# Score levels placed by one wide copy each and a re-ordered start, in a streaming-encoder trunk

## The chip, the cores and the metric

The kernel runs on one core of a Trainium2 chip. The metric is the device time of one execution in microseconds (us), the median of several runs. TensorE is the matmul engine, VectorE and ScalarE the elementwise engines, GpSimd the fourth; the trace calls them PE, DVE, ACT and POOL. SP is the engine that issues most DMAs.

## The reference

Two layers of a streaming encoder on x (512 tokens, 1024 channels) in float32, cut here to what is computed:

```python
for l in range(DEPTH):                      # DEPTH = 2
    x = x + 0.5 * swiglu(rmsnorm(x, ffn1_norm[l]), ffn1_w1[l], ffn1_w3[l], ffn1_w2[l])
    h = rmsnorm(x, mix_norm[l])
    q_a, f_a, i_a, g_a, u_b = jnp.split(h @ w_in[l], splits, axis=-1)
    o_a = hgrn2_mixer(q_a, f_a, i_a, g_a, lb_all[l], hgrn_norm[l])   # gated linear recurrence, 4 heads
    o_b = multiscale_pool(u_b, pool_w[l], pool_scale[l])             # trailing means over 2, 4, 8, 16
    x = x + jnp.concatenate([o_a, o_b], axis=-1) @ w_out[l]
    x = x + mem_cross_attention(rmsnorm(x, xa_norm[l]), rmsnorm(mem, mem_norm[l]), ...)
    x = x + 0.5 * swiglu(rmsnorm(x, ffn2_norm[l]), ffn2_w1[l], ffn2_w3[l], ffn2_w2[l])
return rmsnorm(x, final_norm)
```

The recurrence is S_t = diag(f_t) S_(t-1) + k_t v_t^T with o_t = S_t^T q_t; inside a stretch of tokens it is a masked product of scores with v.

## The kernel before, in words

All activations are held transposed: eight x tiles of 128 channels by 512 tokens. Every matrix operand is split into a high part (`whi`, `h`) and a low part (`wlo`), and a product is three matmuls (`mm3`, lines 84 to 86): high by high, high by low, low by high. `split` (lines 76 to 80) makes the high part on ScalarE and the low part on VectorE.

Weights come in chunks (`Weights`): 512 KB of raw weights are loaded on SP's queue (`load`, line 142), split (`cut`), and used by 24 matmuls of 512 columns. `next` hands out a chunk, cuts those `ahead` (SPLIT = 5 of them) and loads those 7 ahead. Tiles for all this, and for most of the rest, come from one pool of 38 slots (`s_tile`).

The feed-forward networks treat their first chunks plainly and the rest in blocks (`Pairs.block`): two chunks taken together by a scheme with seven products, for which sums of weights are needed. A block's load (lines 128 to 135) is four DMAs on SP's queue and one accumulating DMA on GpSimd's (`wsum`), its cut four splits and two additions (eight slots), and each of its products is closed by a copy on ScalarE (`keep`, line 545). A block counts as two in `ahead`.

At the start, x is loaded in five DMAs with chunk 0 (in halves) and chunk 1 between them. Eleven dummy products (line 1134) run on a tile of ones. `wts.first()` cuts chunk 0, `norm.part(d)` splits each x tile (lines 79 and 80), and `begin` multiplies chunks 0 to 3 with the x tiles, two tiles (a `k2`) at a time; the squares of x (lines 386 and 392), which the norm needs, come from its fourth step on. The norm's row is applied when a PSUM tile is evacuated.

In the mixing stage (`mix`) the scores inside stretches of 128 tokens are built level by level: at level m (1, 2, 4, ... 64) the first half of each stretch of 2m tokens meets the second half. `levels` is a generator that is stepped between weight chunks. At levels 2 to 16 `dense` forms products (line 768) for the two groups g of heads, ScalarE copies them to `packed` (line 777), DMAs on ScalarE's queue put them into `spread` (line 782), which is zero elsewhere, and `place` writes them by `copy_predicated` into the score tile `atd` (line 740), eight instructions of 64 elements for a group. At level 32 eight copies evacuate the products (line 773), at level 64 one for a group (line 816). After each level, `kg` and `qf` are scaled in place for the next one (lines 822 and 824), and a level is placed in the step of group 0 of the next.

The order of the instructions on each engine is set when the kernel is built: a planner walks the program with its own model of time and lets a later instruction go first where an earlier one is not ready.

Of the kernel before, what the change touches and what calls it, by code (L numbers as in the profile page):

```python
# [7 lines left out]
F32 = mybir.dt.float32  # L8
F32R = mybir.dt.float32r
I32 = mybir.dt.int32  # L10
AF = mybir.ActivationFunctionType
ALU = mybir.AluOpType
AX = mybir.AxisListType

P = 128
D = 1024
T = 512
M = 256
L = 2
NK = D // P  # L20
NT = T // P
# [25 lines left out]
def trunk_kernel(ctx: ExitStack, tc: tile.TileContext, ap: dict, out: bass.AP):  # L47
    nc = tc.nc
# [19 lines left out]
    def s_tile(shape, dt, name):  # L68
        return sp.tile(shape, dt, tag="s", name=name)


    def split(hi, lo, src, scale=None):


        if scale is None:
            act.copy(hi, src)  # L76
            dve.tensor_tensor(lo, src, hi.bitcast(F32), op=ALU.subtract)  # L77
        else:
            act.activation(hi, src, AF.Copy, scale=scale)
            dve.scalar_tensor_tensor(lo, src, scale, hi.bitcast(F32), op0=ALU.mult, op1=ALU.subtract)  # L80
# [8 lines left out]
    class Weights:  # L89
# [33 lines left out]
        def load(self, i):  # L123
            if i in self.raw or i in self.hl:
                return
            if len(self.src[i]) == 2:
                c1, c2 = self.src[i]
                s1, t1 = s_tile([P, NK, P], F32, "wsum"), s_tile([P, NK, P], F32, "raw")
                t2 = s_tile([P, 4, P], F32, "raw")
                nc.sync.dma_start(s1[:, :4], c1[:, :4])  # L130
                nc.sync.dma_start(s1[:, 4:], c2[:, :4])
                nc.sync.dma_start(t1, c1)
                nc.sync.dma_start(t2, c2[:, 4:])
                nc.gpsimd.dma_start(s1, c2, accum_op=ALU.add)
                self.raw[i] = [t.rearrange("p a b -> p (a b)") for t in (t1, t2, s1)]
                return
            src, a, b = self.src[i]
            t = s_tile([P, 1024], F32, "raw")
            tv = t[:, :a * b].rearrange("p (a b) -> p a b", b=b)
            for c in range(0, a, a if i else a // 2):  # L140
                ce = c + (a if i else a // 2)
                nc.sync.dma_start(tv[:, c:ce], src[:, c:ce])
            self.raw[i] = t

        def cut(self, i):
# [30 lines left out]
            _, a, b = self.src[i]  # L176
            hi, lo = s_tile([P, 1024], F32R, "whi"), s_tile([P, 1024], F32R, "wlo")
            n = a * b
            step = n if i else n // 2
            for c in range(0, n, step):  # L180
                split(hi[:, c:c + step], lo[:, c:c + step], raw[:, c:c + step])
            self.hl[i] = tuple(t[:, :n].rearrange("p (a b) -> p a b", b=b) for t in (hi, lo))
            yield

# [5 lines left out]
                else:  # L190
                    return

        def first(self):
            self.todo.append(self.cut(0))
            self.step()

        def next(self):
            i = self.at
            self.at += 1
            while self.todo:  # L200
                self.step()
            block = len(self.src[i]) == 2
            ahead = [*self.ahead(i, 4 if block else self.SPLIT)]
            if i + 3 == len(self.src) - 1:
                ahead.append(i + 3)
            for j in ahead:
                if j not in self.hl:
                    self.todo.append(self.cut(j))
                    if not block or j == i:
                        while self.todo:  # L210
                            self.step()
            for j in self.ahead(i, self.LOAD):
                self.load(j)
            return self.hl.pop(i)
# [41 lines left out]
    xT = [xall[:, d] for d in range(NK)]  # L256
    vec = const.tile([P, NV], F32, name="vec")
    nc.scalar.dma_start(vec, ap["vec"])
    for c, ce in ((0, 1), (1, 2), (2, 4), (4, 6), (6, 8)):
        nc.sync.dma_start(xall[:, c:ce], ap["x"][:, c:ce])  # L260
        if c % 2 == 0 and c < 4:
            wts.load(c // 2)

    fixed = const.tile([P, P + 16 + 64 * len(MASKS)], F32, name="fixed")
    nc.sync.dma_start(fixed, ap["fixed"])
# [424 lines left out]
    def mix(l, norm, mem, after):  # L690
# [41 lines left out]

        def place(g, m, rows):

            for hh in range(2):
                o = atd[g][:, hh].rearrange("p i (b e j) -> p i b e j", e=2, j=m)
                src = rows[:, hh * 256:(hh + 1) * 256].rearrange("p (i b j) -> p i b j", i=NT, j=m)
                mk = masks[m].rearrange("p (b j) -> p b j", j=m)
                for i in range(NT):
                    dve.copy_predicated(o[:, i, :, 1, :], mk, src[:, i])  # L740

        keys = [None, None]

# [9 lines left out]
                dst = keys[g][:, hh * HT:(hh + 1) * HT].rearrange("p (i j b) -> p i b j", i=NT, j=m)  # L753
                act.copy(dst, src[:, hh].rearrange("p (i b) j -> p i b j", i=NT))

        spread = s_tile([P, 2, T], F32, "spread")
        pool.memset(spread, 0.0)
        packed = [None]

        def dense(g, m):  # L760
# [17 lines left out]
            if g == 1:  # L778
                n = max(m, 64 // m)
                for x in range(64 // n):  # L780
                    rows = slice(x, P, 2 * m) if m <= 4 else slice(2 * m * x, 2 * m * x + m)
                    nc.scalar.dma_start(spread[rows], packed[0][x * n:(x + 1) * n])

        def levels():

# [7 lines left out]
            for m in (1, 2, 4, 8, 16, 32, 64):  # L793
                nb = T // (2 * m)
                tots = [None, None]
                for g in range(2):
# [19 lines left out]
                        dve.tensor_copy(atd[g][0:64, :, :, 64:128].rearrange("p h i t -> p (h i) t"),  # L816
                                        ps[0:64, :].rearrange("p (x t) -> p x t", t=64))
                    tv = tot[g].rearrange("p h (b e) -> p h b e", e=2)
                    kv = kg[g].rearrange("p h (b e j) -> p h b e j", e=2, j=m)
                    qv = qf[g].rearrange("p h (b e j) -> p h b e j", e=2, j=m)  # L820
                    for hh in range(2):
                        dve.tensor_tensor(kv[:, hh, :, 0, :], kv[:, hh, :, 0, :],
                                          tv[:, hh, :, 1:2].broadcast_to([P, nb, m]), op=ALU.mult)
                        dve.tensor_tensor(qv[:, hh, :, 1, :], qv[:, hh, :, 1, :],
                                          tv[:, hh, :, 0:1].broadcast_to([P, nb, m]), op=ALU.mult)
                    nt_ = s_tile([P, 2, nb], F32, "tot") if m == 1 else sm.tile([P, 2, nb], F32, tag=f"tot{m}", name="tot", bufs=2)
                    dve.tensor_tensor(nt_, tv[:, :, :, 0], tv[:, :, :, 1], op=ALU.mult)
                    tots[g] = nt_
                    if m < 32:
                        first_halves(g, 2 * m)  # L830
                    if g == 0 and 2 < m <= 32:
                        place(0, m // 2, spread[:, 0])
                        place(1, m // 2, spread[:, 1])
                    yield
                tot = tots
            last.extend(tot)
# [293 lines left out]


    idle = ps_tile()
    for _ in range(11):
        pe.matmul(idle[:, :P], ones, ones, start=True, stop=True)
    norm = Norm("ffn1_norm", 0, late=1, rest=0, far=0)
    wts.first()
    for d in range(NK):
        norm.part(d)

    def begin(norm):  # L1140

        ps = [ps_tile(), ps_tile(), acc_tile(), acc_tile()]
        w = {}
        for p, k2 in ((0, 0), (0, 1), (1, 0), (1, 1), (0, 2), (1, 2), (0, 3), (1, 3),
                      (2, 0), (2, 1), (2, 2), (2, 3), (3, 0), (3, 1), (3, 2), (3, 3)):
            if p not in w:
                w[p] = wts.next()
            for k in (2 * k2, 2 * k2 + 1):
                mm3(ps[p], (w[p][0][:, k], w[p][1][:, k]), norm.h[k], start=k == 0, stop=k == NK - 1)
            while norm.n < NK and p + k2 > 1:  # L1150
                norm.square(norm.n)
            if p == 2 and k2 == 2:
                norm.tick()
        return ps
# [80 lines left out]
```

## Time and profile before

| what | us |
|---|---|
| median of 3 runs | 2135.25 (2132.23 to 2136.88) |
| the profiled execution | 2134.99 |
| its span, from the first to the last instruction | 2133.2 |
| TensorE busy | 2106.7 |
| VectorE busy | 1370.6 |
| ScalarE busy | 901.2 |
| GpSimd busy | 225.5 |

The mean granted clock of TensorE over the span is 0.994 of full speed. The clock has two levels, 1.2 and 2.4 GHz, so a mean below 1 over a stretch is a share of it at the lower level. A matmul's row gives its duration from issue to a modelled end; neighbours overlap, so their spacing is read from their starts.

### The profile page before, as it was taken

How to read it: one execution, taken by the hardware profiler on the slowest of the kernel's cores; microseconds unless marked ns; L12 is line 12 of the kernel's file. 1: busy time of each engine (PE TensorE's matmuls, PEld its weight loads, DVE VectorE, ACT ScalarE, POOL GpSimd, SP SyncE). 2: the span in 40 equal slices, each digit the busy share in tenths (PEclk: the TensorE clock that was granted, in tenths of full speed). 3: DMA queues.
4: the chain of work that ended last, by engine and by line, in shares of the span. 5: the costliest groups of instructions: out<-in, count | busy, mean ns of one | idle time of the engine just before them, and what ended most of it. 6: DMA issues, size and time to landing. Idle time of an engine off the chain costs nothing. (4 is left out here: it accounts for less than half of the span.)

```text
span 2133.2 us, 31051 instructions
## 1 busy us (share of the span) xinstructions
PE 2106.7 (99%) x12380; PEld 1858.4 (87%) x12380; DVE 1370.6 (64%) x2104; ACT 901.2 (42%) x1397; POOL 225.5 (11%) x216
## 2 busy tenths in 40 slices
PE   9999999999999999999999999999999999999998
PEld 7889898887988888999988998988789888889896
DVE  6747565687646485755676575658875556657565
ACT  4425345433534343544444353434244443435254
POOL 1100000312000020000011000003110001100002
PEclk9999999999999999999999999999999999999999
DMA  4355465222424245737325745532334331475453
GB/s 176 107 158 149 119 170 167 68 86 95 143 79 138 62 113 144 190 104 193 127 57 151 193 119 164 167 104 73 86 110 133 109 104 50 140 202 133 135 154 117
DMA packets 106866, 271.58 MB, mean 127 GB/s; under 512 B 10592, under 2 KB 10592, under 8 KB 106720
## 3 DMA queue, kind: packets, MB, share of 16 engines
q1 hardware_dynamic: 92944, 227.85, 32.0%
q0 software_dynamic: 11952, 38.02, 10.2%
q10 hardware_dynamic: 1824, 3.73, 0.8%
q8 instruction: 97, 1.59, 0.3%
q14 instruction: 49, 0.40, 0.1%
HBM read 259.85 MB, written 2.10 MB: 123 GB/s over the span
## 5 line engine op out<-in xcount | busy, mean ns | idle before, releaser
L77 DVE TENSOR_TENSOR wlo<-raw,whi 128x1024 fp32r<-128x1024 f32 (+1 forms) x329 | 404.5, 1250 | 81.2 <-ACT whi L76 73.7
L76 ACT CAST whi<-raw 128x1024 fp32r<-128x1024 f32 (+1 forms) x329 | 335.0, 1046 | 118.3 <-DMA raw<-in_ffn_w_dram 57.3
L84 PE MATMUL ps<-h,whi 128*128 128x512 f32 x848 | 333.4, 395 | 5.1 <-DVE atd L773 4.1
L85 PE MATMUL ps<-h,whi 128*128 128x512 f32 x848 | 333.3, 393 | 0.5 <-DVE h L80 0.5
L86 PE MATMUL ps<-h,wlo 128*128 128x512 f32 x848 | 332.0, 392 | 0.4 <-DVE wlo L77 0.4
L84 PE MATMUL ps<-bh,whi 128*128 128x256 f32 x744 | 210.1, 284 | 3.4 <-ACT keep L545 2.8
L84 PE MATMUL acc<-bh,whi 128*128 128x256 f32 x744 | 211.1, 284 | 1.9 <-ACT keep L545 1.9
L85 PE MATMUL acc<-bl,whi 128*128 128x256 f32 x744 | 211.0, 284 | 0.0
L86 PE MATMUL acc<-bh,wlo 128*128 128x256 f32 x744 | 210.9, 284 | 0.0
L86 PE MATMUL ps<-bh,wlo 128*128 128x256 f32 x744 | 210.9, 283 | 0.0
L85 PE MATMUL ps<-bl,whi 128*128 128x256 f32 x744 | 210.8, 283 | 0.0
L77 DVE TENSOR_TENSOR wlo<-wsum,whi 128x1024 fp32r<-128x1024 f32 x124 | 154.9, 1249 | 69.3 <-ACT whi L76 68.1
L76 ACT CAST whi<-wsum 128x1024 fp32r<-128x1024 f32 x124 | 130.1, 1050 | 157.9 <-DVE wsum L164 85.5
L84 PEld LDWEIGHTS ps<-h,whi 128*128 128x128 f32 x848 | 160.9, 190 | 40.0 <-issue 4.3
L85 PEld LDWEIGHTS ps<-h,whi 128*128 128x128 f32 x848 | 160.9, 190 | 35.7 <-DVE h L80 2.5
L86 PEld LDWEIGHTS ps<-h,wlo 128*128 128x128 f32 x848 | 160.8, 190 | 34.5 <-DVE wlo L77 0.8
L84 PEld LDWEIGHTS ps<-bh,whi 128*128 128x128 f32 x744 | 142.6, 192 | 4.3 <-ACT keep L545 3.1
L84 PEld LDWEIGHTS acc<-bh,whi 128*128 128x128 f32 x744 | 143.2, 192 | 2.6 <-ACT keep L545 2.3
L85 PEld LDWEIGHTS acc<-bl,whi 128*128 128x128 f32 x744 | 143.3, 193 | 0.3
L85 PEld LDWEIGHTS ps<-bl,whi 128*128 128x128 f32 x744 | 143.0, 192 | 0.6
L86 PEld LDWEIGHTS acc<-bh,wlo 128*128 128x128 f32 x744 | 143.3, 193 | 0.0
L86 PEld LDWEIGHTS ps<-bh,wlo 128*128 128x128 f32 x744 | 143.0, 192 | 0.0
(262 smaller groups left out, 4295.4 us busy)
## 6 DMA issues: line engine op xcount, KB each, us to landing
raw<-in_ffn_w_dram SPq DMA_DIRECT2D x207, 512.0 KB
wsum<-in_ffn_w_dram SPq DMA_DIRECT2D x124, 256.0 KB
wsum<-in_ffn_w_dram POOLq DMA_DIRECT2D x62, 512.0 KB, 6.3
raw<-in_ffn_w_dram SPq DMA_DIRECT2D x64, 256.0 KB
raw<-in_w_in_dram SPq DMA_DIRECT2D x32, 512.0 KB
raw<-in_w_out_dram SPq DMA_DIRECT2D x16, 512.0 KB
raw<-in_xa_wk_dram SPq DMA_DIRECT2D x16, 512.0 KB
raw<-in_xa_wq_dram SPq DMA_DIRECT2D x16, 512.0 KB
```

What stands on the lines that cost most here:

```text
L76: act.copy(hi, src)
L77: dve.tensor_tensor(lo, src, hi.bitcast(F32), op=ALU.subtract)
L84: pe.matmul(o, a[0], b[0], start=start, stop=False, skip_group_check=more)
L85: pe.matmul(o, a[0], b[1], start=False, stop=False, skip_group_check=more)
L86: pe.matmul(o, a[1], b[0], start=False, stop=stop, skip_group_check=more)
```

## The change

- `load` and `cut` lose the special case of chunk 0. A new `half` loads or splits one half (four of eight row blocks) of a chunk. x is loaded with halves of chunks 0 and 1 between its DMAs, and their splits stand between the splits of x tiles 0 to 3.
- In `begin` the pairs alternate between chunk 0 and chunk 1 from the start, two dummy products stand after each of the first six pairs, and the squares come after the eighth. Thirteen dummies instead of eleven run first.
- `next` cuts 4 ahead instead of 5 as soon as one of the next four entries is a block.
- `place` is one instruction of 512 elements with the mask broadcast, the scalings of `kg` and `qf` take both heads of a group at once, `spread` has two buffers that alternate by level, and a level is placed in the step of group 1 of the next level, not of group 0.

```diff
@@ class Weights
+        def half(self, i, c, what):
+            src, a, b = self.src[i]
+            if i not in self.raw:
+                self.raw[i] = s_tile([P, 1024], F32, "raw")
+                self.hl[i] = tuple(s_tile([P, NK, P], F32R, x) for x in ("whi", "wlo"))
+            t = self.raw[i].rearrange("p (a b) -> p a b", b=b)[:, 4 * c:4 * c + 4]
+            if what == "load":
+                nc.sync.dma_start(t, src[:, 4 * c:4 * c + 4])
+            else:
+                hi, lo = self.hl[i]
+                split(hi[:, 4 * c:4 * c + 4], lo[:, 4 * c:4 * c + 4], t)
+                if c:
+                    self.raw.pop(i)
...
             block = len(self.src[i]) == 2
-            ahead = [*self.ahead(i, 4 if block else self.SPLIT)]
+            near = any(len(x) == 2 for x in self.src[i:i + 4])
+            ahead = [*self.ahead(i, 4 if near else self.SPLIT)]
...
-    for c, ce in ((0, 1), (1, 2), (2, 4), (4, 6), (6, 8)):
+    for c, ce, half in ((0, 1, 0), (1, 2, None), (2, 4, 1), (4, 6, None), (6, 8, None)):
         nc.sync.dma_start(xall[:, c:ce], ap["x"][:, c:ce])
-        if c % 2 == 0 and c < 4:
-            wts.load(c // 2)
+        if half is not None:
+            wts.half(0, half, "load")
+            wts.half(1, half, "load")
...
         def place(g, m, rows):
-            for hh in range(2):
-                o = atd[g][:, hh].rearrange("p i (b e j) -> p i b e j", e=2, j=m)
-                src = rows[:, hh * 256:(hh + 1) * 256].rearrange("p (i b j) -> p i b j", i=NT, j=m)
-                mk = masks[m].rearrange("p (b j) -> p b j", j=m)
-                for i in range(NT):
-                    dve.copy_predicated(o[:, i, :, 1, :], mk, src[:, i])
+            o = atd[g].rearrange("p h i (b e j) -> p (h i) b e j", e=2, j=m)[:, :, :, 1, :]
+            src = rows.rearrange("p (x b j) -> p x b j", x=2 * NT, j=m)
+            mk = masks[m].rearrange("p (o b j) -> p o b j", o=1, j=m).broadcast_to([P, 2 * NT, 64 // m, m])
+            dve.copy_predicated(o, mk, src)
...
-        spread = s_tile([P, 2, T], F32, "spread")
-        pool.memset(spread, 0.0)
+        spreads = [s_tile([P, 2, T], F32, "spread") for _ in range(2)]
+        for t in spreads:
+            pool.memset(t, 0.0)
+        spread = {m: spreads[i % 2] for i, m in enumerate((2, 4, 8, 16))}
...
-                    for hh in range(2):
-                        dve.tensor_tensor(kv[:, hh, :, 0, :], kv[:, hh, :, 0, :],
-                                          tv[:, hh, :, 1:2].broadcast_to([P, nb, m]), op=ALU.mult)
-                        dve.tensor_tensor(qv[:, hh, :, 1, :], qv[:, hh, :, 1, :],
-                                          tv[:, hh, :, 0:1].broadcast_to([P, nb, m]), op=ALU.mult)
+                    dve.tensor_tensor(kv[:, :, 0, :], kv[:, :, 0, :], tx[:, :, 1:2].broadcast_to([P, 2 * nb, m]), op=ALU.mult)
+                    dve.tensor_tensor(qv[:, :, 1, :], qv[:, :, 1, :], tx[:, :, 0:1].broadcast_to([P, 2 * nb, m]), op=ALU.mult)
...
-                    if g == 0 and 2 < m <= 32:
-                        place(0, m // 2, spread[:, 0])
-                        place(1, m // 2, spread[:, 1])
+                    if g == 1 and 2 < m <= 32:
+                        for x in range(2):
+                            place(x, m // 2, spread[m // 2][:, x])
...
-    for _ in range(11):
-        pe.matmul(idle[:, :P], ones, ones, start=True, stop=True)
+    def rest(n):
+        for _ in range(n):
+            pe.matmul(idle[:, :P], ones, ones, start=True, stop=True)
+    rest(13)
     norm = Norm("ffn1_norm", 0, late=1, rest=0, far=0)
-    wts.first()
     for d in range(NK):
         norm.part(d)
+        if d < 4:
+            wts.half(d % 2, d // 2, "split")
...
-        for p, k2 in ((0, 0), (0, 1), (1, 0), (1, 1), (0, 2), (1, 2), (0, 3), (1, 3),
+        for p, k2 in ((0, 0), (1, 0), (0, 1), (1, 1), (0, 2), (1, 2), (0, 3), (1, 3),
...
-            while norm.n < NK and p + k2 > 1:
+            if p < 2 and k2 < 3:
+                rest(2)
+            while norm.n < NK and p + k2 > 3:
                 norm.square(norm.n)
```

## Rows read from the trace of the kernel before

**Rows 1.** The page: busy us (share), instructions of each engine.

```profile
PE 2106.7 (99%) x12380; PEld 1858.4 (87%) x12380; DVE 1370.6 (64%) x2104; ACT 901.2 (42%) x1397; POOL 225.5 (11%) x216
```

**Rows 2.** Waits of TensorE: us in total, times, longest us.

```profile
PE ps L84 <- DVE atd L773: 4.1, 2, 2.0
PE ps L815 <- DVE qf L824: 3.2, 3, 1.1
PE ps L84 <- ACT keep L545: 2.8, 1, 2.8
PE acc L84 <- ACT keep L545: 1.9, 2, 1.0
```

**Rows 3.** Windows: us, each engine's busy us (instructions), TensorE's clock, DMA share, GB/s.

```profile
6.14:22.75 16.61, 15.33 (x48) 10.25 (x49) 14.36 (x24) 15.20 (x22) 0.00 (x0) 0.79 0.99 391
...
160.00:170.00 10.00, 10.00 (x79) 10.00 (x78) 4.09 (x8) 3.83 (x9) 1.72 (x2) 0.91 0.78 217
...
480.00:503.00 23.00, 18.79 (x111) 15.02 (x108) 20.79 (x57) 2.28 (x3) 6.30 (x13) 0.85 0.21 58
...
1530.00:1552.00 22.00, 18.80 (x122) 15.14 (x120) 20.51 (x59) 2.10 (x2) 6.30 (x13) 0.92 0.21 61
```

**Rows 4.** Timeline of TensorE, start: start us, duration us, [wait].

```profile
1.00 4.55 PE L1134 MATMUL ps<-ones 128*128 128x128 f32 x22 [1.00 <-POOL nhalf L277]
6.14 0.49 PE L84 MATMUL ps<-h,whi 128*128 128x512 f32 x1 [0.59 <-ACT h L79]
...
8.24 0.78 PE L84 MATMUL ps<-h,whi 128*128 128x512 f32 x1 [0.41 <-ACT h L79]
```

**Rows 5.** Timeline of ScalarE at the start.

```profile
7.47 0.72 ACT L79 ACTIVATE h<-xall,vec 128x512 fp32r<-128x512 f32 x1 [0.86 <-DMA xall<-in_x_dram]
...
11.63 1.33 ACT L79 ACTIVATE h<-xall,vec 128x512 fp32r<-128x512 f32 x2 [0.21 <-DMA xall<-in_x_dram]
...
15.13 1.04 ACT L76 CAST whi<-raw 128x1024 fp32r<-128x1024 f32 x1
```

**Rows 6.** Groups of VectorE, 0 to 24 us: busy us, mean ns, idle.

```profile
L80 DVE SCALAR_TENSOR_TENSOR h<-xall,vec,h 128x512 fp32r<-128x512 f32 x8 | 5.8, 746 | 0.8 <-ACT h L79 0.6
L392 DVE TENSOR_TENSOR sq<-sq 128x512 f32<-128x512 f32 x7 | 4.8, 684 | 0.2
```

**Rows 7.** Timelines of SP, GpSimd, ScalarE, TensorE at the first block entry.

```profile
142.38 0.33 SPq L130 DMA_DIRECT2D wsum<-in_ffn_w_dram  x1
...
147.14 0.86 POOL L134 DMA_DIRECT2D wsum<-in_ffn_w_dram  x1 [14.08 <-DVE xall L436]
...
156.34 1.04 ACT L76 CAST whi<-wsum 128x1024 fp32r<-128x1024 f32 x1 [5.96 <-issue]
157.29 0.64 ACT L545 COPY keep<-ps 128x256 f32<-128x256 f32 x2
...
157.70 0.39 PE L84 MATMUL ps<-bh,whi 128*128 128x256 f32 x1 [2.85 <-ACT keep L545]
```

**Rows 8.** TensorE after level 64, layer 0: first, last half-clock product.

```profile
494.06 0.77 PE L84 MATMUL ps<-h,whi 128*128 128x512 f32 x1 [2.04 <-DVE atd L773]
...
499.74 0.44 PE L85 MATMUL ps<-h,whi 128*128 128x512 f32 x1
```

**Rows 9.** Timelines of VectorE and ScalarE, levels 4 to 16 of layer 0.

```profile
457.64 2.27 DVE L740 COPY_PREDICATED atd<-fixed,spread 128x64 f32<-128x64 int32 x16 [1.87 <-DMA spread<-packed]
...
474.27 0.57 ACT L777 COPY packed<-ps 64x512 f32<-64x512 f32 x1
...
476.24 4.20 DVE L740 COPY_PREDICATED atd<-fixed,spread 128x64 f32<-128x64 int32 x16 [1.08 <-DMA spread<-packed]
...
480.51 2.46 ACTq L782 DMA_DIRECT2D spread<-packed  x4
```

**Rows 10.** Groups of VectorE in layer 0's mixing, and line 824's min/median/max ns.

```profile
L801 DVE TENSOR_TENSOR atd<-ps,fixed 128x512 f32<-128x512 f32 x4 | 2.6, 678 | 0.0
...
L824 DVE TENSOR_TENSOR qf<-qf,tot x48: 402/416/1264, 442.3 to 1551.2; 128x256 f32<-128x256 f32 x48
```

More of the change, by code (lines that the diff above doesn't have):

```diff
@@ L139, in load @@
             tv = t[:, :a * b].rearrange("p (a b) -> p a b", b=b)
-            for c in range(0, a, a if i else a // 2):
-                ce = c + (a if i else a // 2)
-                nc.sync.dma_start(tv[:, c:ce], src[:, c:ce])
+            nc.sync.dma_start(tv, src)
             self.raw[i] = t
@@ L178, in cut @@
             n = a * b
-            step = n if i else n // 2
-            for c in range(0, n, step):
-                split(hi[:, c:c + step], lo[:, c:c + step], raw[:, c:c + step])
+            split(hi[:, :n], lo[:, :n], raw[:, :n])
             self.hl[i] = tuple(t[:, :n].rearrange("p (a b) -> p a b", b=b) for t in (hi, lo))
@@ L191, in step @@
                     return
-        def first(self):
-            self.todo.append(self.cut(0))
-            self.step()
+        def half(self, i, c, what):
[11 more added lines that the diff above has]
+                    self.raw.pop(i)
         def next(self):
@@ L781, in dense @@
                     rows = slice(x, P, 2 * m) if m <= 4 else slice(2 * m * x, 2 * m * x + m)
-                    nc.scalar.dma_start(spread[rows], packed[0][x * n:(x + 1) * n])
+                    nc.scalar.dma_start(spread[m][rows], packed[0][x * n:(x + 1) * n])
         def levels():
@@ L818, in levels @@
                     tv = tot[g].rearrange("p h (b e) -> p h b e", e=2)
-                    kv = kg[g].rearrange("p h (b e j) -> p h b e j", e=2, j=m)
-                    qv = qf[g].rearrange("p h (b e j) -> p h b e j", e=2, j=m)
-                    for hh in range(2):
-                        dve.tensor_tensor(kv[:, hh, :, 0, :], kv[:, hh, :, 0, :],
-                                          tv[:, hh, :, 1:2].broadcast_to([P, nb, m]), op=ALU.mult)
-                        dve.tensor_tensor(qv[:, hh, :, 1, :], qv[:, hh, :, 1, :],
-                                          tv[:, hh, :, 0:1].broadcast_to([P, nb, m]), op=ALU.mult)
+                    kv = kg[g].rearrange("p h (b e j) -> p (h b) e j", e=2, j=m)
+                    qv = qf[g].rearrange("p h (b e j) -> p (h b) e j", e=2, j=m)
+                    tx = tot[g].rearrange("p h (b e) -> p (h b) e", e=2)
+                    dve.tensor_tensor(kv[:, :, 0, :], kv[:, :, 0, :], tx[:, :, 1:2].broadcast_to([P, 2 * nb, m]), op=ALU.mult)
+                    dve.tensor_tensor(qv[:, :, 1, :], qv[:, :, 1, :], tx[:, :, 0:1].broadcast_to([P, 2 * nb, m]), op=ALU.mult)
                     nt_ = s_tile([P, 2, nb], F32, "tot") if m == 1 else sm.tile([P, 2, nb], F32, tag=f"tot{m}", name="tot", bufs=2)
```

## The prediction

> **What bounds the kernel now.** I read the shares of the page first: TensorE is busy for 2106.7 us of the 2133.2 us span [rows 1]. So the kernel is bound by TensorE, and the order of the views follows from that: not the costliest groups, but TensorE's own waits, then the stretches in which its clock is below full, because a product issued at the lower of the two levels (1.2 GHz) takes twice as long and still counts as busy. The waits [rows 2] name three places and no more: the level part of the mixing stage (products queued behind the evacuation of line 773, 4.1 us, and behind the scaling of line 824, 3.2 us), and the entry into the block products (behind the copies of line 545, 2.8 and 1.9 us). The windows [rows 3] show that the clock drops at the same places and at one more: from the first product at 6.14 to 22.75 us, where 48 products stand in 16.6 us at a mean clock of 0.79. A full-clock spacing can be read from [rows 8]: 13 products start between 494.06 and 499.74 us at half clock, 0.44 us each, so 0.22 us at full. Whatever an edit does to VectorE, ScalarE or the queues counts only if it moves one of these places.
>
> The queues are ordered by a planner that fills idle places by its own idea of time, with program order as priority: the first product of chunk 1 comes in program order before the third pair of chunk 0, but the cast of chunk 1 stands at 15.13 us [rows 5], behind all of x. Exact orders after the change can't be read from this trace; I price work and dependences, and keep the ends for the range.
>
> **Part 1, the start.** Forty-eight products at 0.22 us would need 10.6 us; they take 16.6, so 6.0 us lie here, in waits and half clock. The cause is in the arrivals: ScalarE waits for x tile 1 until 7.47 and for tiles 4 and 5 until 11.63 [rows 5]. With chunk 0 alone each x tile gives only three products; with a half of chunk 1 beside it, six. The change loads as many bytes ahead of each x tile as before (half of chunk 1 instead of the second half of chunk 0 before tile 1, the two second halves instead of chunk 1 before tiles 4 and 5), so I leave the arrivals where they are; the one DMA issue that is added on SP shifts the last two x loads, `fixed` and chunks 2 on by one issue, hidden behind transfers that run at a DMA share of 0.99 [rows 3]. Chunk 0 and 1's splits cost nothing new. Taking the squares out: seven additions of 0.68 us each on VectorE, 4.8 us [rows 6], no longer stand among the eight products of 0.75 us that make the low halves of x. They are now due after the first eight pairs, where VectorE and ScalarE have only the splits of chunks 2 to 4 to do; what waits for them is the row of the norm, needed when the fifth PSUM tile of that pool is wanted, two chunks of 24 products later, so I price their move at nothing. If that cover is gone, TensorE waits for at most the 4.8 us of additions.
>
> Dummies: two more ahead (13 instead of 11) and twelve between. Eleven took 4.55 us in 22 records [rows 4], 0.41 each at half clock, about 0.21 at full. The two ahead end at about 6.4 us instead of 5.6, 0.24 us behind the first product of before. The twelve are 2.5 us at full and 5.0 at half clock. In gaps they are free; if all of them stand between ready products, TensorE ends the 48 at 6.4 + 10.6 + 2.5 = 19.5 us, 3.2 us ahead of 22.75; if all are in gaps, at 17.0, a gain of 5.7. The mean of 0.79 over 16.6 us is 7.0 us at half clock, from about 8.24, where a product took 0.78 us [rows 3, 4], to 15.2. If the clock is at half up to there again, the 8.8 us from 6.4 hold 20 of the 60 products and the other 40 need 8.8: 24.0, a loss of 1.2. I take a gain of 3.5, near the case of full clock with dummies in the way, since the first products at 6.14 still ran at full clock after the dummies.
>
> A rule of the Trainium skill speaks against the dummies: the page "TensorE: Matmul & The Clock Gate", section "The mechanism", says that products start and end strictly in the order of the program. No row here shows a dummy ahead of a ready product; by this rule each misplaced one costs its whole length, which is the 19.5 us case and not the 17.0 us one.
>
> **Part 2, the entry into blocks (`near`).** With two plain chunks left ahead of the blocks, `ahead(i, 5)` cut the second block at once; now it is cut one chunk later. Going through the other distances (one, three, four chunks) both limits yield the same list. There are eleven entries (two in the first network, three in each of the others). What moves is the order of eight slots for the second block's parts against three slots for the third block's load. In before the third block's loads are issued at 142.38 and its accumulating DMA at 147.14; the cast of it, 156.34, ends 5.96 us of idle time on ScalarE, the copies queued behind it come at 157.29, and TensorE waits until 157.70 [rows 7]. That is 2.85 us, with at least 0.9 us of half clock after it (0.91 over the 10 us after 160 [rows 3]); two more entries wait 1.9 us in all [rows 2]. 5.7 us in sum. With its slots first, the third load can go before the burst. The price is that the second block's splits come up to a chunk (24 x 0.22 = 5.3 us) later. I take a gain of 3.0; ends: 5.7, and a loss of 3.8 (the same stall once more at an entry that has none now). I stay below the middle of the gain because the transfer, not the issue, may be what is late.
>
> **Part 3, the levels.** A placing of 64 elements: sixteen took 2.27 us back to back [rows 9], 0.14 each. One of 512 elements is not in the trace; the nearest row is line 801's, 512 elements for 0.68 us [rows 10]; the other end is eight times 0.14, 1.1, no gain. I take 0.65, since 64 elements at that row's rate are more than half of 0.14. Ten placings a layer then save about 0.5 us each, 5 us of VectorE a layer, two of the five levels in the critical stretch. The merged scalings: 256 elements at a median of 0.416 [rows 10] against 0.68 for 512, about 0.1 us saved for each pair, under 1 us in that stretch. More important are two dependences. One `spread` buffer forces the DMA of level 16 to wait for the placing of level 8: that runs from 476.24 for 4.20 us and the four DMAs are issued at 480.51, with everything on ScalarE's queue behind them [rows 9]. With two buffers they can go right after the copy to `packed`. And the last placing (level 16, two groups, 16 instructions) comes in program order after both evacuations of level 32 and their scalings instead of before the second group's; these are what TensorE waits for [rows 2].
>
> So about 2 us of placing leave the way of the evacuations, 2 us are saved by width, and the wait for the DMA goes: more than the 2.04 us ahead of 494.06 [rows 8] and the two waits of about 1.1 before it [rows 2]. In layer 0 4.2 us of waits and 13 x 0.22 = 2.8 us of half clock hang on it; in layer 1 3.1 us (the rest of lines 773 and 824 in [rows 2]) and, scaled by the clock lost in the two windows (0.08 against 0.15 of nearly equal lengths [rows 3]), 1.5 us. Sum 11.6. What is late next is VectorE itself: 20.8 of 23.0 us busy from 480 to 503 [rows 3]; with some 4 us saved it has 16.8 us of work for the 16.0 that are left without the waits and the half clock, so the transposes after level 64 may wait. I leave 1.6 us a layer for that: gain 8.4, ends 0 and 11.6. The second `spread` takes one of 38 slots during levels 2 to 8; the trace shows no TensorE wait for weights there, so nothing, with the rival below as its cost.
>
> The page "SBUF — State Buffer", section "Who interferes with whom", says that a VectorE instruction with two SBUF inputs and a GpSimd instruction that reads SBUF shut each other out for a whole instruction. The placing that took 4.20 instead of 2.27 us [rows 9] agrees. By it a wide placing could be held as long as a narrow one and hold GpSimd four times as long, which alters no term above.
>
> **Sum.** 3.5 + 3.0 + 8.4 = 14.9 us off the profiled execution's 2134.99: 2120.1. That execution lies 0.26 us under the median of the three runs, so I give 2120.
>
> **Rivals.** (a) VectorE stays the bound in the levels: a wide placing costs near 1.1, or the wait moves to the transposes. Then half of the 8.4 goes, with the half clock; start and entry give 3: about 2128. For it: VectorE at 90%. Against: the order alone takes the last placing out of the way. (b) The parts do not do what they say: dummies stand in front of ready products at half clock (-1), entries unchanged (0), levels 2: about 2134. (c) Slower: the later cut of the second block, with one slot fewer in the mixing stage, makes ScalarE's copies queue behind a late cast at entries that now run clean. Each such stall costs 3.8 us [rows 2, 3]; it decides from the point where the second block's first pieces come later than its first product. With half the gains kept (7.5), two of the eight clean entries cancel it, and from there it is slower; with four, 4 x 3.8 - 7.5 = 7.7, about 2143. For it: ScalarE is strictly queued, and three entries show the stall. Against: in the others the splits are done well ahead and nothing waits. (d) All three places clear wholly: 5.7 + 5.7 + 11.6 = 23.0: 2112.
>
> **How the numbers follow.** Forecast (2114 to 2125) 0.53, (d) 0.09, (a) 0.19, (b) 0.11, (c) 0.08. Range: from (d)'s 2112 to 2133, which takes in (a) and the near end of (b). A change under 0.2% (4.3 us) can't be told from none by a measurement of this kernel. Faster: forecast, (d), (a) with a little lost to its near side, 0.80; same: (b) and what (a) loses, 0.12; slower: 0.08.
>
> **What would show it.** The profile after: 48 products done by 17 to 20 us at a clock near 1.0; no wait of TensorE over 1 us behind lines 773 and 824's successors, clock 1.0 in both level stretches; DMAs of `spread` issued right after the copies to `packed`; placings of about 0.65 us; the copies of line 545 not behind a late cast. The forecast is wrong if placings cost 1.1, if the clock at the start stays near 0.8, or if new waits for low halves of weights appear at the entries.

## The result and the profile after

The changed kernel takes 2116.68 us (median of 4 runs, 2115.53 to 2117.18) where the kernel before took 2134.47 (4 runs, 2132.23 to 2136.88). The ratio is 0.9916, with a 95% interval of 0.9899 to 0.9933: 17.8 us, or 0.8%, faster. The profiled execution took 2116.26 us with a span of 2114.5, 18.7 us shorter than the span before.

I read the views of the new profile in the same order as before. First the page's line of busy times, then the waits of TensorE (us in total, times, longest us):

```profile
PE 2099.7 (99%) x12408; PEld 1856.3 (88%) x12408; DVE 1353.2 (64%) x1909; ACT 901.3 (43%) x1398; POOL 235.1 (11%) x218
```

```profile
PE ps L854 <- DVE u L924: 2.9, 2, 1.5
PE ps L1144 <- POOL nhalf L286: 1.0, 1, 1.0
PE acc L84 <- ACT whi L76: 1.0, 1, 1.0
PE ps L863 <- ACT kt L856: 0.5, 2, 0.2
```

All four waits of [rows 2] are gone. One is new: the transposes (line 854) wait twice, 2.9 us in all, behind the instruction on VectorE that makes the tile `u` (line 924). The kernel's lines have moved by 7 to 10; the old lines 773, 815, 824, 545 and 740 are now 782, 824, 832, 554 and 747. The windows at the three places (columns as in [rows 3]):

```profile
6.00:20.00 14.00, 14.00 (x75) 12.18 (x74) 12.77 (x27) 12.27 (x20) 0.00 (x0) 1.00 1.02 401
480.00:500.00 20.00, 18.40 (x115) 14.39 (x114) 16.21 (x32) 5.93 (x13) 4.58 (x6) 1.00 0.32 108
1520.00:1540.00 20.00, 18.22 (x112) 14.08 (x111) 17.97 (x35) 5.59 (x11) 6.91 (x11) 1.00 0.31 103
```

The clock is 1.00 in all three, against 0.79, 0.85 and 0.92 in [rows 3].

**The start**, TensorE's timeline:

```profile
1.00 7.14 PE L1144 MATMUL ps<-ones 128*128 128x128 f32 x36 [1.00 <-POOL nhalf L286]
7.89 0.48 PE L84 MATMUL ps<-h,whi 128*128 128x512 f32 x1
...
20.50 0.39 PE L84 MATMUL acc<-h,whi 128*128 128x512 f32 x1
```

The 48 products end where the first one into `acc` begins: 20.50 us, against 22.97 in the trace of before. TensorE never waits in between. Eleven dummies left 22 records before [rows 4]; 36 records are 18 dummies, so not thirteen but eighteen ran ahead: the planner pulled five of the later twelve forward.

**The entry into the blocks**, timelines of SP's queue, GpSimd and ScalarE, the instructions that answer to [rows 7]:

```profile
127.12 0.38 SPq L130 DMA_DIRECT2D wsum<-in_ffn_w_dram  x1
...
134.41 0.86 POOL L134 DMA_DIRECT2D wsum<-in_ffn_w_dram  x1 [3.85 <-DMA wsum<-in_ffn_w_dram]
...
147.24 1.05 ACT L76 CAST whi<-wsum 128x1024 fp32r<-128x1024 f32 x1
148.48 0.37 ACT L554 COPY keep<-ps 128x256 f32<-128x256 f32 x1 [0.20 <-PE ps L86]
```

The third block's load is issued at 127.12 instead of 142.38, its accumulating DMA at 134.41 instead of 147.14, and its cast runs at 147.24 with no wait instead of at 156.34. The copies behind it follow at once.

**The levels** of layer 0, timelines of ScalarE's queue, VectorE and TensorE:

```profile
467.30 2.47 ACTq L791 DMA_DIRECT2D spread<-packed  x4
...
466.88 1.81 DVE L747 COPY_PREDICATED atd<-fixed,spread 128x512 f32<-128x512 int32 x2 [0.27 <-DMA spread<-packed]
475.31 0.97 DVE L782 COPY atd<-ps 32x128 f32<-32x128 f32 x4
479.49 1.33 DVE L747 COPY_PREDICATED atd<-fixed,spread 128x512 f32<-128x512 int32 x2
483.92 1.54 DVE L831 TENSOR_TENSOR kg<-kg,tot 128x512 f32<-128x512 f32 x1
489.62 0.68 DVE L924 TENSOR_TENSOR u<-ps,rrow 128x512 f32<-128x512 f32 x1
...
490.36 0.55 PE L854 MATMUL ps<-fixed,kg 128*128 128x128 f32 x3 [1.36 <-DVE u L924]
```

The DMAs of level 16 are issued right after the copy to `packed`, at 467.30 instead of 480.51 [rows 9]; the placing of level 8 takes 1.81 us instead of 4.20; and the last placing (479.49) stands behind the evacuations of level 32.

By place, the trace gives: start 22.97 - 20.50 = 2.5; entries 5.7, the waits and half clock that the prediction counted there; levels 4.1 + 3.2 us of waits and the 4.3 of half clock that it estimated, less the 2.9 of the new wait, 8.7. That is 16.9 of the 18.7 us. Of the other 1.8, 1.3 stood at the first entry too, in two rows of before that the 5.7 leaves out, a product and a window:

```profile
145.97 0.39 PE L84 MATMUL ps<-bh,whi 128*128 128x256 f32 x1 [0.52 <-DVE xall L436]
150.00:160.00 10.00, 7.15 (x54) 6.95 (x53) 3.97 (x6) 2.59 (x6) 0.86 (x1) 0.92 1.05 300
```

TensorE waits 0.5 us ahead of the long wait, and the clock is down before 160 as well: 0.92 over 10 us is 0.8 us. So the entries held 7.0 us, the three places 18.2, and 0.5 I have not placed.

### The profile page after: what moved, and what is told of

Same layout as the page of the kernel before. It is cut to its first block, busy times and chain, and to the rows that moved or that the text cites. A ratio compares the mean times of both kernels' runs of the same rounds, so it can differ in the third digit from the quotient of the medians.

```text
span 2114.5 us, 30902 instructions
## 1 busy us (share of the span) xinstructions
PE 2099.7 (99%) x12408; PEld 1856.3 (88%) x12408; DVE 1353.2 (64%) x1909; ACT 901.3 (43%) x1398; POOL 235.1 (11%) x218
```

## Experiments

B is the kernel before, A the changed kernel.

| kernel | median us (runs) | lowest to highest | ratio to before, 95% interval |
|---|---|---|---|
| p_start: B + start | 2132.34 (11) | 2129.22 to 2134.51 | 0.9995 [0.9987, 1.0004] |
| p_entry: B + entry | 2127.56 (7) | 2127.24 to 2128.60 | 0.9974 [0.9964, 0.9984] |
| p_levels: B + levels | 2124.37 (8) | 2120.95 to 2131.82 | 0.9961 [0.9946, 0.9976] |
| b_loadfirst: B, third load first | 2128.35 (10) | 2126.98 to 2130.73 | 0.9979 [0.9969, 0.9988] |
| n_start: A without start | 2118.71 (5) | 2118.03 to 2119.23 | 0.9927 [0.9914, 0.9940] |
| a_11ahead: A, dummies ahead only | 2116.15 (4) | 2115.45 to 2118.71 | 0.9922 [0.9909, 0.9935] |
| a_narrow: A, narrow placings | 2121.49 (4) | 2119.52 to 2122.60 | 0.9942 [0.9925, 0.9958] |
| a_early: A, placing a step earlier | 2116.01 (4) | 2115.31 to 2117.35 | 0.9919 [0.9904, 0.9934] |
| a_onespread: A, one buffer | 2125.35 (4) | 2123.65 to 2125.49 | 0.9960 [0.9945, 0.9975] |
| x_oneearly: A, one buffer, placing a step earlier | 2122.72 (5) | 2121.72 to 2122.94 | 0.9945 [0.9932, 0.9957] |
| x_act64: A, level 64 on ScalarE | 2114.20 (5) | 2113.08 to 2114.75 | 0.9905 [0.9891, 0.9920] |
| x_act64_one: and level 1 copied | 2114.39 (4) | 2113.55 to 2117.54 | 0.9918 [0.9901, 0.9934] |

The kernel before, run beside them, had medians of 2132.09 to 2134.26.

### One part at a time

**p_start** is the kernel before with the change's new `half`, order of pairs, dummies and later squares:

```diff
-    for _ in range(11):
-        pe.matmul(idle[:, :P], ones, ones, start=True, stop=True)
+    rest(13)
...
-        for p, k2 in ((0, 0), (0, 1), (1, 0), (1, 1), (0, 2), (1, 2), (0, 3), (1, 3),
+        for p, k2 in ((0, 0), (1, 0), (0, 1), (1, 1), (0, 2), (1, 2), (0, 3), (1, 3),
```

> The kernel before with the start alone changed. Theory (the three parts act each at its own place and their gains add): the 48 products of chunks 0 and 1 end at 20.5 us instead of 22.75, as in the changed kernel, and the median falls by 2 to 2.5 us; the waits in the levels (4.1 and 3.2 us) and behind line 545's copies (4.7 us) stay. Rival (the entries into blocks were cleared by the earlier start, which gives the loads more lead, and not by the limit of 4): the 2.85 us wait at the first entry shrinks or goes here already, and the median falls by 5 us or more.

It gained 0.9 us (2133.24 - 2132.34), and the interval reaches from 2.8 gained to 0.9 lost. The waits of TensorE that stay:

```profile
PE ps L823 <- DVE qf L832: 4.9, 3, 2.7
PE ps L84 <- DVE atd L781: 3.6, 2, 2.0
PE ps L84 <- ACT keep L553: 3.0, 2, 2.3
```

The levels and the first entry wait as before. In the trace the first product into `acc` begins at 20.43, 2.5 us earlier than before, but the runs differ by more than that: 5.3 us between its runs, 8.0 us between 21 runs of the kernel before beside it. The median of this run can't size the start.

**p_entry** is one line:

```diff
-            ahead = [*self.ahead(i, 4 if block else self.SPLIT)]
+            near = any(len(x) == 2 for x in self.src[i:i + 4])
+            ahead = [*self.ahead(i, 4 if near else self.SPLIT)]
```

> The kernel before with the limit of 4 alone (the second block cut one chunk later). Theory: the three waits behind line 545's copies go (2.85, 1.03, 0.86 us and the half clock after the first), no other wait comes, and the median falls by 5 to 6 us. Rival (the start did it): the first wait stays near 2.85 us and the median moves by less than 2 us.

5.7 us (2133.24 - 2127.56), what [rows 2, 3, 7] put there. Its waits of TensorE:

```profile
PE ps L84 <- DVE atd L774: 4.1, 2, 2.0
...
PE ps L84 <- ACT keep L546: 0.3, 1, 0.3
```

The copies are ready now, but for 0.3 us, and the levels wait as they did. A small wait is new, 0.8 us at the transposes of layer 0. The clock behind the level waits is not as it was: in layer 0 the same 2.0 us wait is followed by full clock (1.00 from 490 to 500, where before had 0.66), so the half clock behind a wait is no fixed price. And the runs lie within 1.4 us of each other instead of 8.0.

**p_levels** has the wide placing, the merged scalings, the second `spread` and the later placing:

```diff
+            o = atd[g].rearrange("p h i (b e j) -> p (h i) b e j", e=2, j=m)[:, :, :, 1, :]
+            dve.copy_predicated(o, mk, src)
...
+        spreads = [s_tile([P, 2, T], F32, "spread") for _ in range(2)]
...
+                    if g == 1 and 2 < m <= 32:
```

> The kernel before with the levels alone changed (wide placing, two spread buffers, merged scalings, placing in group 1's step). Theory: the waits behind lines 773 and 824 go, about 1.4 us of wait a layer stays at the transposes after level 64, the clock is full in both layers' level stretch, and the median falls by 8 to 10 us. Rival (the gain in the levels needs the ScalarE time or the slots that the other parts free): waits of over 2 us stay there and the median falls by less than 6 us.

8.9 us (2133.24 - 2124.37) by medians, with single runs from 2120.95 to 2131.82 and an interval of 5.1 to 11.5. The profiled one was 2128.89:

```profile
PE acc L84 <- ACT keep L545: 3.9, 2, 2.1
PE ps L845 <- DVE u L915: 2.7, 2, 1.4
PE ps L84 <- ACT keep L545: 2.6, 2, 1.5
```

The level waits have become 2.7 us at the transposes, near the changed kernel's 2.9; the entries, untouched here, wait 6.5 us where the profile of before had 4.7. The three parts alone add up to 0.9 + 5.7 + 8.9 = 15.5 us, near the 16.6 of the whole against the same median.

**n_start** takes the start out of the changed kernel instead (the lines of p_start, undone), where the runs scatter less.

> The changed kernel without its start part: block entries and levels as changed, the start as before (chunk 0 in halves, squares among the low halves, eleven dummy products, none between). What is the start worth in the company of the other two? Theory: the 2.5 us by which TensorE begins the second kind of product earlier (20.50 instead of 22.97 us) are kept to the end, because no later wait of TensorE is on a transfer any more: 2116.7 + 2.5 = about 2119.2, and 20 to 30 us shows no difference in clock. Rival: it is worth what it was alone, 0.9 us, because waits further on take the gain back: about 2117.6. In both the first product into acc comes near 23.0 us.

2118.71 against 2116.68: the start is worth 2.0 us, and the ranges don't overlap. The first product into `acc` came at

```profile
23.44 0.39 PE L84 MATMUL acc<-h,whi 128*128 128x512 f32 x1
```

which is 2.9 us later than in the changed kernel; 0.9 of that does not show in the median. The theory's 2.5 is nearer than the rival's 0.9.

### Which piece of the start: the dummies

```diff
-    rest(13)
+    rest(11)
...
-            if p < 2 and k2 < 3:
-                rest(2)
```

> The changed kernel with eleven dummy products ahead, as before, and none between the pairs. Theory (the dummies between hold the clock up while TensorE waits for x): the first product starts at about 6.0 instead of 7.89 us, but the clock falls to half from about 8 us on and the 48 products end at 21.5 to 24 us instead of 20.5; the median rises by 1 to 3 us over the changed kernel's. Rival (the dummies between only cost, since the planner puts five of them ahead of the first product and the interleaving alone keeps TensorE busy): the clock stays near full, the 48 products end at 18 to 19 us and the median falls by about 2 us.

Nothing changed: 2116.15 against 2116.68. TensorE's timeline shows why:

```profile
1.00 5.07 PE L1144 MATMUL ps<-ones 128*128 128x128 f32 x22 [1.00 <-POOL nhalf L286]
...
8.35 1.01 PE L84 MATMUL ps<-h,whi 128*128 128x512 f32 x2 [1.14 <-ACT h L79]
...
14.88 0.50 PE L85 MATMUL ps<-h,whi 128*128 128x512 f32 x1 [0.68 <-DVE h L80]
...
20.00 0.39 PE L84 MATMUL acc<-h,whi 128*128 128x512 f32 x1
```

The first product starts at 5.84 instead of 7.89 us, then 1.1 and 0.7 us are waited for pieces of x, and the end is at 20.00. The granted clock from 10 us on is 1.00 without dummies between. So the dummies fill time in which x isn't there yet; what this kernel keeps of the part, the halves of two chunks, the alternating pairs and the later squares, does the work. Which of these three was not tried.

### Which piece of the entry: the slot order

In the kernel before, the third block's load is put ahead of the second block's cut, whose time stays:

```diff
+            if not block and [len(x) for x in self.src[i:i + 4]] == [3, 3, 2, 2]:
+                for j in self.ahead(i, self.LOAD):
+                    self.load(j)
             for j in ahead:
```

> The kernel before, with one thing moved at an entry into blocks: two plain chunks ahead of the blocks, the third block's load takes its three slots ahead of the second block's cut, which stays where it was. Theory (the order of the slots is what the limit of 4 changes): the waits behind line 545's copies go as with the limit of 4 alone, and the median falls by 5 to 6 us. Rival (the later cut itself is what helps, by leaving ScalarE and VectorE to the last plain chunks): the 2.85 us wait stays and the median moves by less than 2 us.

5.0 us (2133.39 - 2128.35) of the 5.7. GpSimd's and ScalarE's timelines:

```profile
137.10 0.86 POOL L134 DMA_DIRECT2D wsum<-in_ffn_w_dram  x1 [3.38 <-DMA wsum<-in_ffn_w_dram]
...
149.94 1.05 ACT L76 CAST whi<-wsum 128x1024 fp32r<-128x1024 f32 x1
```

The accumulating DMA is out 10 us earlier than in [rows 7] and the cast waits for nothing. At this first entry, what was late was the issue of the load: in before the queue waits 12.8 us ahead of it, until an addition of the second block's cut (line 164) is done. But the copies still hold TensorE elsewhere:

```profile
PE ps L84 <- ACT keep L548: 1.8, 2, 1.0
```

These are two later entries, at 791.48 and 1140.71, the ones at which before waits 1.03 and 0.86 us. There only two blocks follow the plain chunks, so there is no third block's load to bring forward, and the loads of the two are issued 14.8 us apart in before, in b_loadfirst and in p_entry alike. p_entry clears both waits, so at these entries it is the later cut that helps, and the theory held at the first entry alone. How the later cut does it was not looked into.

### Which piece of the levels: width, order, second buffer

**a_narrow** puts the eight narrow copies of 64 elements back into `place`:

```diff
-            dve.copy_predicated(o, mk, src)
+            for hh in range(2):
...
+                for i in range(NT):
+                    dve.copy_predicated(o[:, i, :, 1, :], mk, src[:, i])
```

> The changed kernel with eight narrow placings in place of a wide one. Each group's placing from spread then takes about 1.15 instead of 0.72 us, that of level 1 the same (1.31 to 1.35 us either way). Theory (VectorE sets the end of the level stretch): the waits at the transposes after level 64 (1.4 and 1.5 us) grow by 1 to 2 us a layer and the median rises by 2 to 5 us. Rival (the order alone clears the stretch and VectorE has room): the median rises by less than 1 us.

4.8 us are lost (2121.49 - 2116.68). Waits of TensorE, then a window:

```profile
PE ps L856 <- DVE u L926: 3.4, 2, 1.7
PE ps L865 <- DVE atd L827: 2.5, 2, 1.3
```

```profile
480.00:500.00 20.00, 17.05 (x97) 13.17 (x96) 16.41 (x43) 5.07 (x11) 4.18 (x6) 0.91 0.33 107
```

A second wait stands behind the evacuation of level 64 (line 827), and the clock falls to 0.91: VectorE sets the end of this stretch, so width counts.

**a_early** places a level in the step of group 0 of the next, as before:

```diff
-                    if g == 1 and 2 < m <= 32:
+                    if g == 0 and 2 < m <= 32:
```

> The changed kernel with the placing of a level back in the step of group 0 of the next one. Theory (order is the main thing): TensorE waits again behind the evacuation of level 32 or the scaling after it, 2 to 4 us in both layers with half clock after it, and the median rises by 3 to 6 us. Rival (width and the second buffer are enough): the median rises by less than 1 us.

2116.01: no difference. The later step is worth nothing that shows, once a placing is short and the buffer is free. The test is half a one: in VectorE's timeline one of the two placings of level 16 moved ahead of the evacuations of level 32 (473.01), and the planner left the other behind them (479.71).

**a_onespread** keeps the changed order but has one `spread` again:

```diff
-        spreads = [s_tile([P, 2, T], F32, "spread") for _ in range(2)]
+        spread = s_tile([P, 2, T], F32, "spread")
```

> The changed kernel with one spread buffer. Theory (the order of the placing is what clears the levels; the second buffer only frees ScalarE's queue): the DMAs of level 16 are issued again behind the placing of level 8, but no wait of TensorE over 1 us comes back before the transposes, and the median rises by 0 to 2 us. Rival (the second buffer is the key): waits of 2 us or more a layer come back and the median rises by 4 to 7 us.

8.7 us are lost (2125.35 - 2116.68). But this is no clean undo: with the late step, the DMA of a level stands ahead of the placing of the level before, so this kernel places the next level's scores, and each placing waits for a DMA that it needn't wait for. Its loss can't be put down to the buffer alone. So **x_oneearly** takes one buffer and the early step together, the placing of the kernel before with wide copies:

> The changed kernel with one spread buffer and each level placed in the step of group 0 of the next level, as in the kernel before, so that the placing has the right scores; the wide placing and merged scalings stay. Theory (the second buffer is what lets the DMA of a level go): the DMAs of level 16 wait for the placing of level 8 as in the kernel before, the evacuations of level 32 on VectorE come later, and a good part of the wait of TensorE comes back, though the wide placing shortens it by about 2 us: 2121 to 2124. Rival (width is enough): the placing of level 8 now takes 1.8 us instead of 4.2, so the DMA that waits for it is early enough, and it comes out within 1.5 us of the changed kernel: 2115 to 2118.

2122.72, a loss of 6.0 us against the changed kernel, and of 6.7 against a_early, from which it differs by the buffer alone. ScalarE's queue and the wait of TensorE:

```profile
470.37 2.46 ACTq L789 DMA_DIRECT2D spread<-packed  x4
```

```profile
PE ps L822 <- DVE qf L830: 5.4, 3, 3.0
```

The DMAs wait until 470.37 for the placing of level 8 (468.13 to 470.3) instead of going at 467.30. All that hangs on them is 3 to 5 us late: the placing of level 16, the casts behind them on ScalarE, the scalings before level 64. Width alone is not enough. Width (4.8) and buffer (6.0) are more in sum than the 8.9 of the part; that each needs the other would explain it, but no run takes both away.

### What is late next

In the changed kernel VectorE is busy for 9.9 of the 10 us from 480 while ScalarE is idle for 7.4 us. **x_act64** moves the two evacuations of level 64 over:

```diff
-                        dve.tensor_copy(atd[g][0:64, :, :, 64:128].rearrange("p h i t -> p (h i) t"),
+                        act.copy(atd[g][0:64, :, :, 64:128].rearrange("p h i t -> p (h i) t"),
```

> The changed kernel with the two evacuations of level 64 on ScalarE instead of VectorE. In the changed kernel VectorE is busy for 9.90 of the 10 us from 480, ScalarE idle for 7.4 us from 480.1, and TensorE waits 1.36 us (layer 0) and 1.5 us (layer 1) for a row of u that is queued on VectorE behind those two copies of 0.68 us. Theory (VectorE is what is late now): u comes up to 1.2 us earlier a layer, TensorE waits for at most 0.3 us, 2.0 to 2.6 us gained in all: about 2114.3. Rival (the row of u is late for another reason, its products or the queue's order): no gain, 2116 to 2117.5, and the wait stays over 1 us.

2114.20: 2.5 us below the changed kernel, and the fastest version run. Timelines of ScalarE and TensorE:

```profile
480.09 0.58 ACT L825 COPY atd<-ps 64x512 f32<-64x512 f32 x1 [0.51 <-PE ps L824]
...
488.65 0.55 PE L854 MATMUL ps<-fixed,kg 128*128 128x128 f32 x3 [0.16 <-DVE u L924]
```

The wait behind `u` fell from 2.9 to 0.5 us in all. This trace has a wait that the changed kernel's has not, 0.98 us behind a copy of `keep` at 1824.81, the entry of the last network.

**x_act64_one** also copies the products of level 1 to SBUF before they are placed, to see why these four placings take twice the time of the other sixteen.

```diff
-                        place(g, m, ps)
+                        one = s_tile([P, T], F32, "one")
+                        act.copy(one, ps)
+                        place(g, m, one)
```

> The version with the level 64 evacuations on ScalarE, and in it the products of level 1 copied from PSUM to SBUF by ScalarE before they are placed, so that the four placings of level 1 read SBUF as the sixteen others do. In the changed kernel a placing of 512 elements takes 0.72 us from SBUF (levels 2 to 16) and 1.345 us from PSUM (level 1). Theory (the source in PSUM makes it slow): the four placings of level 1 now take 0.70 to 0.75 us. Rival (level 1's pattern, every second element of the score tile and the mask, makes it slow): they stay at 1.3 us or more. On the time both give no difference, 2113.5 to 2115, since TensorE waits for nothing in the stretch of level 1.

The line's groups of the changed kernel, then of this one (minimum, median and maximum ns, first and last start):

```profile
L747 DVE COPY_PREDICATED atd<-fixed,spread x16: 700/723/1541, 441.2 to 1523.8; 128x512 f32<-128x512 int32 x16
L747 DVE COPY_PREDICATED atd<-fixed,ps x4: 1323/1345/1354, 420.4 to 1470.5; 128x512 f32<-128x512 int32 x4
```

```profile
L747 DVE COPY_PREDICATED atd<-fixed,one x4: 1314/1838/2360, 419.4 to 1470.0; 128x512 f32<-128x512 int32 x4
```

My theory fell: from SBUF two take 1.31 us, and two 2.36, these while GpSimd ran an operation beside them (at 427.44 and 1469.54). So PSUM as the source does not make them slow; what is left is level 1's pattern, every second element alone. Whether the score tile's pattern or the mask's does it was not tried. The time stays (2114.39), as both expected.

## Why the prediction was right, and where not

The forecast was 2120.0 with a range of 2112 to 2133; the time is 2116.7. The sum of 14.9 us stood against 18.7 in the profiled execution and 17.8 by the medians. By its steps:

- **What bounds the kernel: right.** The three places named by [rows 2, 3] hold 18.2 of the 18.7 us, and in the changed kernel's trace no other place has gained a wait.
- **Start, 3.5: too high.** It is 2.5 in the trace and 2.0 by n_start. Full clock was right (1.00). The 3.5 stood near the case of 19.5 us, and the end came at 20.50. The starting point of that case, "the two ahead end at about 6.4", was wrong: eighteen dummies ran ahead, and the first product came at 7.89, 1.5 us late; that only seven stood between gave 0.8 back. But an earlier beginning buys little: a_11ahead, with the first product at 5.84, ends at 20.00. The step that failed is therefore "if all are in gaps, at 17.0", the near end of the term: it counted TensorE's work alone, and the pieces of x arrive too late for that, even with six products from each.
- **Squares: the reason failed, the price held.** I wrote that they "no longer stand among the eight products" of the low halves. VectorE's timeline after still has them there, since the planner puts them into idle places:

```profile
9.90 0.69 DVE L401 TENSOR_TENSOR sq<-sq 128x512 f32<-128x512 f32 x1
10.50 1.41 DVE L80 SCALAR_TENSOR_TENSOR h<-xall,vec,h 128x512 fp32r<-128x512 f32 x2
11.83 0.68 DVE L401 TENSOR_TENSOR sq<-sq 128x512 f32<-128x512 f32 x1
```

  No wait of TensorE follows from it.
- **The strict order of products.** The trace after has dummies between products, and a_11ahead, without them, is as fast. The rule of the Trainium skill ("TensorE: Matmul & The Clock Gate", "The mechanism") would have made a misplaced dummy cost its length. No run here shows it: those between stand where x is awaited, and the others were pulled ahead.
- **Entry, 3.0: too low.** It is 5.7 by p_entry, the far end of my range, and 7.0 in the trace. The step that failed is "the transfer, not the issue, may be what is late": b_loadfirst, which moves the issue alone, got 5.0, and the rows at 127.12, 134.41 and 147.24 show that the transfer had time enough. The trace of before could have told me: the second block's load is issued at 127.74, the third's only at 142.38 [rows 7]. The far end was itself too low, since "at least 0.9 us of half clock" was read from 160 on only. And "the order of eight slots for the second block's parts against three slots for the third block's load" is the reason at the first entry alone; the 1.9 us of the other two went with the later cut, whose delay I had counted only as a price.
- **Levels, 8.4: right in size** (8.7 in the trace; 8.9 alone, with an interval of 5.1 to 11.5). Of its reasons, the second buffer (6.0 by x_oneearly) and the width (4.8 by a_narrow) hold. The order, "the last placing comes after both evacuations", did not show: a_early, which takes half of it back, lost nothing. A wide placing takes 0.72 us, near the 0.65 taken, and not the 1.1 of the other end; but the four of level 1 take 1.345 where eight narrow ones from PSUM had taken 1.31 together (at 428.73 in the trace of before), so that only eight of ten placings a layer gain.
- **What is late next: right.** I left 1.6 us a layer for transposes that wait for VectorE; it is 1.4 and 1.5, and x_act64 shows that VectorE's queue is the cause.
- **The lock between VectorE and GpSimd.** I said that it alters no term. Two scalings of 0.68 us on the way to `u` took 1.5 us each (483.92 above is one), while GpSimd ran the additions of line 927. That agrees with the Trainium skill ("SBUF — State Buffer", "Who interferes with whom"), and about 1.7 us of layer 0's queue ahead of the new wait are this. The sum came out since I had left that wait a price, not since the lock was counted.
- **The rivals.** (a) came half true: the wait did move to the transposes, but at full clock. (b) and (c) did not show: no product of the changed kernel's trace waits at an entry (x_act64's has one wait of 0.98 us there). (d) cleared the entries, not the start or the levels.

The three misses had both signs: 1.0 to 1.5 too much for the start, 4.0 too little for the entries in the trace (2.7 by p_entry), 0.3 to 0.5 too little for the levels. In the trace they add up to 3.3 of the 3.8 us between the sum of 14.9 and the 18.7; the rest is the 0.5 that I have not placed. That the misses partly cancel is luck.

## What to carry over

When TensorE is busy for 99% of the time, price its waits and the half clock behind each, place by place, the waits as the firmer part; where a row shows how late an issue is against the transfer's own time, take the full price and don't shade it. Before moving work in program order, ask whether a planner will move it back: some squares stood among the low halves again, and the late placing and the dummies between were worth nothing that shows, while a second buffer, a wide placing, a load ahead of a burst of slots and an evacuation on an idle engine were. Undo each piece in the changed kernel rather than add it to the old one: there the runs of a kernel scattered by 1.2 to 4.0 us, not by 8.0.

## What was not expected of the hardware

- `copy_predicated` of 512 float32 elements takes 0.72 us where runs of two or more elements are placed, and about 1.31 to 1.35 us where every second element is, from PSUM and, in two of four cases, from SBUF; the other two from SBUF took 2.36 us, with an operation of GpSimd beside them.
- The scatter between runs came in large part from the block entries: 8.0 us between 21 runs of the kernel before, 1.4 us between 7 runs with the entry line alone; 10.9 us for p_levels, 1.2 us for n_start, which is p_levels with that line. Why the entries differ from run to run was not looked into.
